# Ten merge gates computed between the mixers and kept in DRAM, with the first block of each layer and the change of layers reordered, in a two-layer hybrid backbone

## The chip, the cores and the metric

The kernel runs on one core of one Trainium2 chip. The metric is the device time of one execution in microseconds (us). A TensorE product of two float32 numbers is made of three products of rounded halves here: each operand is split into a rounded part (H) and the residue (L), and H·H, H·L and L·H are summed in PSUM.

## The reference, cut to what matters

512 latent tokens and 256 context tokens of width 1024 pass two layers. Each layer does the following; the last layer leaves the context alone after the mixers.

```python
shift, scale, gate = _modulation(c, w_ada, b_ada)      # silu(cond) @ w_ada + b_ada
h = _rms_norm(x, norm_g) * (1.0 + scale) + shift       # the same for the context, with c_ctx
(... gla ..., ... hgrn ..., ... attention ..., mg) = _split_in(jnp.matmul(h, w_in))
# three mixers: chunked GLA (4 heads), chunked HGRN (8 heads), windowed attention (8 heads)
y = jnp.stack(ys, axis=2)
proj = jnp.einsum('btnw,nwd->btnd', y, w_branch)       # one projection per branch
gates = jax.nn.sigmoid(mg.reshape(mg.shape[:-1] + (N_BRANCH, D_MODEL)))
merged = jnp.sum(gates * proj, axis=2)
x_new = x + gate * jnp.matmul(merged, w_out)
```

The 24 gates of a layer (3 branches of 8 blocks of 128 channels) depend on h alone. A branch projection depends on all of its mixer's output y.

## The kernel before

The activations lie transposed, channels on the 128 partitions and tokens in the free dimension: 8 blocks of 128 channels by 768 tokens (512 latent, then 256 context). `hH` and `hL` hold the normalized, modulated input of a layer. The weights come as 304 blocks of 128 output channels (512 KB each): `wload` (L704) brings a block into one of three `raw` buffers, `wsplit` (L710) writes its two halves into one of three places of `wring`, and `take` and `ahead` (L762, L772) issue this for up to three blocks ahead of the product. `proj_T` (L782) is one block's projection: 24 products of 512 columns for the latents and, where the context is needed, 24 of 256 columns. `proj_V` (L800) makes token-major values.

**The order of the work** is written out by `make_plan` (L74) as a list of jobs, which the loop at the end of `build` runs one after the other. A job named x is the function `j_x`. In a layer: `start`, the four GLA heads, four pairs of HGRN heads, the attention (values `av`, keys `ak`, then for each of four pairs of heads two queries `aq`, two gate projections `ag` and `arun`), then the merge. The merge goes branch by branch. `mg` (L1643) is a gate: a projection of h and a sigmoid into a buffer. `yload` (L1636) queues the loads of that branch's y, which the mixers have stored in DRAM. `yneed` (L1656) waits until they are loaded and split. `br` (L1663) is a branch projection, multiplied by its gate and added up in `merged`. Branch 0 has its eight gates, then eight branch projections; branches 1 and 2 have four and four, twice. After that come eight `out` jobs (L1710) with the residual sum, which also gather the sum of squares for the next layer.

**Queues.** Every engine works off its instructions in the order in which the program issues them. All loads and stores are issued on SyncE's (SP's) queue, a store (`Emit.store`, L386) as well as a load (`Emit.load`, L376). The mixers' recurrences and attention blocks (`rec_head` L927, `att_block` L1213) are background generators. `pace` (L675) advances them while a projection is issued: it keeps estimated times for each engine (`Emit`, L301) and steps a generator as long as VectorE's or ScalarE's estimate is less than 3 us ahead of TensorE's. A step that needs a buffer when none may be had (`Slots`, L267, 40 buffers of 768 columns, with a reserve for work that has begun) forces other generators on (`on_full`, L682); `need` (L692) does so until one is done. The y loads (`yload_`, L1620) are generators in the same queue, behind the attention blocks.

**Activation tables.** Exp and Ln share one table; Silu and Sigmoid have others. `Emit.act` (L406, instruction at L420) counts a change of table, and loads appear in the trace as ACT_TABLE_LOAD at L402 or L420.

**The beginning** (`j_start` L1329, layer 0). The modulation of block k needs `cond_mm(k)` (L1366, a product of the conditioning with 1 MB of weights), a copy out of PSUM, and `cond_cols(k)` (L1380, a product with two columns, then two small sums on VectorE). Then `make_h` (L906) makes `hH` and `hL` of the block: for the latents and then for the context a scaled product (stt, L447), an activation into `hH` (L420) and another stt into `hL` (L447). The blocks' turns are interleaved so:

```python
for k in range(KT):
    cond_mm(k + 2)
    products(k)          # both weight blocks, latents and context
    cond_cols(k + 2)
    make_h(l, k + 2, xs[k + 2], rs)
```

**The change of layers.** Of the modulation of layer 1, 20 of the 24 blocks are made during the merge of layer 0 on VectorE: a job `adp` puts a weight block of `w_ada` into the stream of weights, and `ada_dots` (L747) forms its dot products with the conditioning (L502). Blocks 16 to 19 are made after the last `out` by four `ads` jobs (L1691): 8 products of two columns each (`ada_mm`, L860), two passes a product. Between them stand the root of the sum of squares (`SumSq.rstd`, L898) and `make_h` of the first five blocks. `j_start` of layer 1 makes the other three, splits the value weights of the first GLA head (`split_v`, L1422) and does the first key and query projections; `j_gvl` (L1466) then uses these value weights.

## Time and profile before

| | us |
|---|---|
| median of 3 runs | 2730.41 |
| lowest, highest | 2730.09, 2734.94 |
| the profiled execution | 2726.76 |
| its span | 2725.0 |
| TensorE busy (PE) | 2634.3, 97% |
| its weight loads (PEld) | 2333.5, 86% |
| VectorE busy (DVE) | 1762.1, 65% |
| ScalarE busy (ACT) | 1104.0, 41% |
| GpSimd busy (POOL) | 169.9, 6% |

The profiled execution is one run, and its span is the part of it between the first and the last instruction. Busy time counts from an instruction's start to its end; matmuls overlap in the pipeline, so their durations are longer than their spacing. A wait in square brackets behind an instruction is the idle time of its engine before it and what ended it. PEclk is the granted clock of TensorE as a share of 2.4 GHz.

### The profile page before, as it was taken

To read this page: it belongs to the slowest core of one execution; us is meant where nothing else is said; L and a number is where in the kernel's file an instruction comes from. 1 tells how busy PE (TensorE), PEld (TensorE's weight loads), DVE (VectorE), ACT (ScalarE), POOL (GpSimd) and SP (SyncE) were. 2 spreads that over 40 slices of the span, in tenths; PEclk is the share of its full clock that TensorE was granted. 3 is DMA by queue.
4 is the path that set the end of the run, shared out by engine and by line. 5 is a ranking of instruction groups with operands and counts; after the bars stand their busy time and mean duration, and the time that the engine had idled before them with its cause. 6 is when DMAs were issued, how large, how long until landed. Compare 5 with 4: busy or idle time off the path is not lost. (4 is left out here: it accounts for less than half of the span.)

```text
span 2725.0 us, 40634 instructions
## 1 busy us (share of the span) xinstructions
PE 2634.3 (97%) x16050; PEld 2333.5 (86%) x16050; DVE 1762.1 (65%) x3562; ACT 1104.0 (41%) x2029; POOL 169.9 (6%) x425
## 2 busy tenths in 40 slices
PE   7999999999999999999999899999999899979998
PEld 5999989988988888888888798888989788868886
DVE  5566657686787766854555456667787887754454
ACT  4444433444334555211211344445565446652122
POOL 0000002001020100000000000001001110000000
PEclk9999999999999999999999899999999999989999
DMA  7111111111111112542423311212121122124333
GB/s 257 48 58 59 59 59 49 57 50 64 59 41 51 45 52 78 173 155 93 139 85 124 124 51 59 74 55 67 59 76 53 45 68 76 63 66 140 102 116 108
DMA packets 87038, 221.91 MB, mean 81 GB/s; under 512 B 9664, under 2 KB 31168, under 8 KB 86848
## 3 DMA queue, kind: packets, MB, share of 16 engines
q1 hardware_dynamic: 86848, 219.32, 24.1%
q8 instruction: 126, 2.06, 0.3%
q14 instruction: 64, 0.52, 0.1%
HBM read 199.36 MB, written 19.92 MB: 80 GB/s over the span
## 5 line engine op out<-in xcount | busy, mean ns | idle before, releaser
L514 PE MATMUL acc<-hH,wring 128*128 128x512 f32 (+1 forms) x5056 | 1398.8, 356 | 8.9 <-ACT hH L420 7.5
L514 PEld LDWEIGHTS acc<-hH,wring 128*128 128x128 f32 x5056 | 897.7, 190 | 137.5 <-ACT hH L420 11.6
L514 PE MATMUL acc<-hL,wring 128*128 128x512 f32 (+1 forms) x2528 | 882.6, 351 | 0.0
L514 PEld LDWEIGHTS acc<-hL,wring 128*128 128x128 f32 x2528 | 478.9, 190 | 57.4 <-DVE hL L447 1.3
L514 PE MATMUL mx<-s,s 128*128 128x256 f32 (+4 forms) x2576 | 397.2, 302 | 26.2 <-ACT s L462 8.7
L514 PEld LDWEIGHTS mx<-s,s 128*128 128x128 f32 (+1 forms) x2576 | 354.1, 195 | 47.8 <-ACT s L462 11.1
L431 DVE TENSOR_TENSOR wring<-raw,wring 128x1024 fp32r<-128x1024 f32 x268 | 329.3, 1234 | 28.6 <-ACT wring L462 19.1
L514 PE MATMUL acc<-s,wring 128*128 128x512 f32 (+1 forms) x1728 | 334.6, 355 | 2.4 <-POOL s L431 1.4
L514 PEld LDWEIGHTS acc<-s,wring 128*128 128x128 f32 x1728 | 286.2, 190 | 49.4 <-POOL s L431 2.6
L420 ACT ACTIVATE s<-s 128x768 f32<-128x768 f32 (+1 forms) x318 | 258.6, 822 | 137.6 <-DVE s L447 88.1
L514 PE MATMUL acc<-wring,hH 128*128 128x256 f32 x1536 | 286.4, 285 | 0.0
L462 ACT CAST wring<-raw 128x1024 fp32r<-128x1024 f32 x167 | 173.3, 1047 | 277.1 <-PE acc L514 237.5
L431 DVE TENSOR_TENSOR s<-s,s 128x768 f32<-128x768 f32 (+4 forms) x278 | 232.0, 851 | 63.8 <-ACT s L420 42.8
L514 PEld LDWEIGHTS acc<-wring,hH 128*128 128x128 f32 x1536 | 242.3, 192 | 0.3
L514 PE MATMUL acc<-wring,hL 128*128 128x256 f32 x768 | 217.2, 283 | 0.0
L420 ACT ACTIVATE s<-acc 128x768 f32<-128x768 f32 (+2 forms) x112 | 76.5, 683 | 275.0 <-PE acc L514 250.3
L431 DVE TENSOR_TENSOR s<-s,fb 128x128 f32<-128x128 f32 (+2 forms) x610 | 183.3, 359 | 0.7
L460 DVE CAST wring<-raw 128x1024 fp32r<-128x1024 f32 x109 | 75.6, 694 | 129.1 <-PE acc L514 127.7
L514 PEld LDWEIGHTS acc<-wring,hL 128*128 128x128 f32 x768 | 147.3, 192 | 0.2
L462 ACT COPY s<-mx 128x256 f32<-128x256 f32 (+2 forms) x191 | 67.5, 378 | 191.2 <-PE mx L514 132.6
L530 PE MATMUL mx<-const,s 128*128 128x128 f32 (+1 forms) x732 | 112.9, 279 | 26.5 <-DVE s L431 16.4
L431 DVE TENSOR_TENSOR s<-s,acc 128x768 f32<-128x768 f32 (+1 forms) x48 | 39.4, 820 | 139.8 <-PE acc L514 139.8
(110 smaller groups left out, 2200.7 us busy)
## 6 DMA issues: line engine op xcount, KB each, us to landing
raw<-in_W SPq DMA_DIRECT2D x304, 512.0 KB, 3.3
y<-s SPq DMA_DIRECT2D x80, 128.0 KB, 1.7
s<-y SPq DMA_DIRECT2D x24, 384.0 KB, 5.9
s<-in_xT SPq DMA_DIRECT2D x16, 384.0 KB, 4.5
s<-in_wada SPq DMA_DIRECT2D x16, 384.0 KB, 7.2
s<-y SPq DMA_DIRECT2D x24, 256.0 KB, 4.6
y<-s SPq DMA_DIRECT2D x80, 64.0 KB, 1.6
s<-in_wvl SPq DMA_DIRECT2D x8, 288.0 KB, 7.1
```

The lines of the kernel that those rows point to most:

```text
L420: self.nc.scalar.activation(out, in_, func, **kw)
L431: (self.nc.vector if e == 'v' else self.nc.gpsimd).tensor_tensor(out, a, b, op=op)
L460: self.nc.vector.tensor_copy(out, in_)
L462: self.nc.scalar.copy(out, in_)
L514: self.nc.tensor.matmul(out, lhsT=lhsT, rhs=rhs, start=start, stop=stop)
L530: self.nc.tensor.transpose(out, in_, ident)
```

## The change

- Gates: a new job `mgx` computes a gate as `mg` does, stores the result in DRAM on SP's queue and frees the buffer. In layer 0, gates 0 and 1 of branch 0 stand between the queries and the gate projections of the third and the fourth pair of attention heads, one each. In layer 1, gates 0 to 3 of branch 0 stand before the attention values, and 4 to 7 two each in the third and fourth pair. `yneed` loads them back.
- Merge: in layer 1 the eight gates of branch 1 now stand before the projections of branch 0, four gates of branch 2 before the eight projections of branch 1, and the first half of branch 2 has no gates before it. In layer 0 the order is as before without the two gates; the y loads of branch 0 come first.
- All 24 modulation blocks of layer 1 are made by dot products in the merge of layer 0; the `ads` jobs, their weights (`wads`) and `ada_mm` go. Two dot blocks stand behind each of the first eight branch projections, one behind each of the others.
- `make_h` is divided into `make_h1` (both scaled products, in place, then both activations) and `make_h2` (both residues), which is issued one block later. In layer 0 a block's products are divided by weight block, with the modulation product of block k+2 between.
- The last `out` of layer 0 makes its latents first, with their sum of squares and root while TensorE makes the context; `start` of layer 1 does all eight blocks of the latents, then of the context. The value weights are loaded and split during the last four `out` jobs.
- Loads at the beginning: a weight block, a modulation block, a weight block, then the rest; the value weights stand ahead of the third weight block. The sum of squares is closed once less.

```diff
+    def mgx(l, nd):
+        job(l, 'mgx', nd, win('mg', 8 * nd[0] + nd[1]))
...
+        early = [(0, d) for d in range(2 if ctx else 8)]
+        spilled = set(early)
+        if not ctx:
+            for _ in range(4):
+                mgx(l, early.pop(0))
...
+            for _ in range(0 if p < 2 else 1 if ctx else 2):
+                mgx(l, early.pop(0))
...
+        cond = [(l, i) for i in range(16, 24)] + [(l + 1, i) for i in range(24)] if ctx else []
+        if ctx:
+            steps = [(0, [(0, d) for d in range(8)], range(8)), (1, [(1, d) for d in range(4)], range(4)),
+                     (1, [(1, d) for d in range(4, 8)], range(4, 8))]
+        else:
+            steps = [(0, [(1, d) for d in range(8)], range(8)), (1, [(2, d) for d in range(4)], range(8))]
+        steps += [(2, [(2, d) for d in range(4)], range(4)), (2, [(2, d) for d in range(4, 8)], range(4, 8))]
+        gated, begun = set(spilled), set()
+        for br, gates, ds in steps:
+            for nd in gates:
+                if nd not in gated:
+                    gated.add(nd)
+                    job(l, 'mg', nd, win('mg', 8 * nd[0] + nd[1]))
+                if br not in begun:
+                    begun.add(br)
+                    job(l, 'yload', br)
+            if br not in begun:
+                begun.add(br)
+                job(l, 'yload', br)
+            job(l, 'yneed', (br, ds))
+            for d in ds:
+                job(l, 'br', (br, d), (f'br{br}', d))
+                for _ in range(2 if len(cond) > 16 else 1):
+                    if cond:
+                        adp(*cond.pop(0))
+            if ds[-1] == 7:
+                job(l, 'yfree', br)
...
+        def part(self, j, q, r):
+            t0, m = self.parts[j]
+            mm(self.ps[j], ones, q[:, t0:t0 + m], start=False, stop=True)
+            if r is not None:
+                self.root(j, r)
+        def root(self, j, r):
+            t0, m = self.parts[j]
+            act(r[:, t0:t0 + m], self.ps[j], AF.Ln, scale=1.0 / D, bias=eps)
+            act(r[:, t0:t0 + m], r[:, t0:t0 + m], AF.Exp, scale=-0.5)
         def rstd(self):
             self.close(True)
-            r = self.acc
-            for ps, (t0, m) in zip(self.ps, self.parts):
-                act(r.ap[:, t0:t0 + m], ps, AF.Ln, scale=1.0 / D, bias=eps)
-            act(r.ap, r.ap, AF.Exp, scale=-0.5)
-            return r
-    def make_h(l, k, x, r):
-        t = arena.alloc(NT)
-        for j, (t0, n) in enumerate(((0, NL), (NL, NC))):
-            sl = slice(t0, t0 + n)
-            shift = ada[l][:, k, j:j + 1]
-            stt(t.ap[:, sl], x.ap[:, sl], amod[l][:, k, j:j + 1], r.ap[:, sl], ALU.mult, ALU.mult)
-            act(hH[k][:, sl], t.ap[:, sl], AF.Identity, bias=shift, scale=1.0)
-            stt(hL[k][:, sl], t.ap[:, sl], shift, hH[k][:, sl].bitcast(F32), ALU.add, ALU.subtract)
-        t.free()
-        x.free()
+            for j in range(len(self.parts)):
+                self.root(j, self.acc.ap)
+            return self.acc
...
+    PARTS = ((0, NL), (NL, NC))
+    def make_h1(l, k, x, r, parts=(0, 1)):
+        for j in parts:
+            sl = slice(PARTS[j][0], sum(PARTS[j]))
+            stt(x.ap[:, sl], x.ap[:, sl], amod[l][:, k, j:j + 1], r.ap[:, sl], ALU.mult, ALU.mult)
+        for j in parts:
+            sl = slice(PARTS[j][0], sum(PARTS[j]))
+            act(hH[k][:, sl], x.ap[:, sl], AF.Identity, bias=ada[l][:, k, j:j + 1], scale=1.0)
+    def make_h2(l, k, x, parts=(0, 1)):
+        for j in parts:
+            sl = slice(PARTS[j][0], sum(PARTS[j]))
+            stt(hL[k][:, sl], x.ap[:, sl], ada[l][:, k, j:j + 1], hH[k][:, sl].bitcast(F32), ALU.add, ALU.subtract)
+        if 1 in parts:
+            x.free()
...
             for k in range(KT):
+                if k < 2:
+                    wload(st['loaded'])
+                    st['loaded'] += 1
                 load(k)
+            load_v(l)
...
+                sq.add(x.ap, k in (1, 3, 5))
...
+        if l == 0:
+            for k in range(KT):
+                make_h2(l, k, xs[k])
+                if k == 1:
                     load_rest()
+                if k == KT - 1:
+                    ahead()
+                products(k, js=(0,))
                 if k + 2 < KT:
                     cond_mm(k + 2)
-            elif k + 5 < KT:
-                make_h(l, k + 5, xs[k + 5], rs)
-            if k == 3:
-                load_v()
-            if k == KT - 1:
-                ahead()
-            if k >= 4:
-                split_v()
-            products(k)
-            if l == 0 and k + 2 < KT:
-                cond_cols(k + 2)
-                make_h(l, k + 2, xs[k + 2], rs)
+                products(k, js=(1,))
+                if k + 2 < KT:
+                    cond_cols(k + 2)
+                    make_h1(l, k + 2, xs[k + 2], rs)
+                if k >= 3 and raw_v:
+                    split_v()
+        else:
+            tail = S0.pop('tail')
+            for part in range(2):
+                make_h1(l, 0, xs[0], rs, (part,))
+                if part == 0:
+                    tail[0]()
+                for k in range(KT):
+                    if k + 1 < KT:
+                        make_h1(l, k + 1, xs[k + 1], rs, (part,))
+                    make_h2(l, k, xs[k], (part,))
+                    if part and k == KT - 1:
+                        ahead()
+                    products(k, (part,))
+                    if part == 0 and k in (0, 2):
+                        tail[1 + k // 2]()
...
+    def j_mgx(l, nd):
+        j_mg(l, nd)
+        s = S_['sig'].pop(nd)
+        S_['spill'][nd] = t = tc.dram_tile([P, S_['nt']], F32, name=f"g{l}_{nd[0]}_{nd[1]}")
+        nc.sync.dma_start(out=t, in_=s.ap)
+        s.free()
...
+    def j_yneed(l, arg):
+        n, ds = arg
+        for d in ds:
+            if (n, d) in S_['spill']:
+                S_['sig'][n, d] = s = arena.alloc(S_['nt'])
+                E.load(s.ap, S_['spill'].pop((n, d)))
...
+        if ctx and d == KT - 1:
+            return last_out(l, d, xr)
+        if ctx and d == 3:
+            load_v(l + 1)
         ps = proj_T(take(), hH, hL, ctx)
+        if ctx and d > 3:
+            split_v()
...
+    def last_out(l, d, xr):
+        sq = S0['sq']
+        i = take()
+        psA, psB = acc()[:, 0:NL], mx()[:, 0:NC]
+        q, r = arena.alloc(NT), arena.alloc(NT)
+        E.t['pe'] = max(E.t['pe'], wready[i])
+        def residual(j, ps):
+            t0, m = PARTS[j]
+            x = xr.ap[:, t0:t0 + m]
+            stt(x, ps, ada[l][:, 16 + d, j:j + 1], x, ALU.mult, ALU.add)
+            act(q.ap[:, t0:t0 + m], x, AF.Square)
+        for j, ps in enumerate((psA, psB)):
+            t0, m = PARTS[j]
+            k = 0
+            for kt in range(KT):
+                for w, x in ((WH(i), hH), (WH(i), hL), (WL(i), hH)):
+                    mm(ps, w[:, kt], x[kt][:, t0:t0 + m], start=(k == 0), stop=(k == 3 * KT - 1))
+                    k += 1
+                if j == 0 and kt == 1:
+                    ahead()
+                if j == 1 and kt == 4:
+                    sq.part(0, q.ap, r.ap)
+            if j == 0:
+                E.table(COMBINED)
+                residual(0, psA)
+                split_v()
+                sq.close()
+        def square():
+            residual(1, psB)
+        def total():
+            sq.part(1, q.ap, None)
+            q.free()
+        def norm():
+            sq.root(1, r.ap)
+        S0['tail'] = square, total, norm
+        S0['rs'] = r
+        x_in[l + 1].append(xr)
```

## Rows read from the trace of the kernel before

**Rows 1.** Busy time in stretches: stretch, length, busy per engine (instructions), clock, DMA, GB/s
```profile
0.00:61.26 61.26, 47.26 (x283) 28.95 (x283) 35.12 (x76) 28.89 (x50) 0.20 (x4) 0.97 0.76 277
...
870.00:1100.00 230.00, 221.21 (x1457) 198.51 (x1456) 157.91 (x363) 124.44 (x295) 14.35 (x6) 0.99 0.19 61
1100.00:1518.90 418.90, 418.90 (x2411) 370.67 (x2409) 238.78 (x448) 69.97 (x78) 0.00 (x0) 1.00 0.39 133
1518.90:1564.14 45.24, 36.26 (x170) 28.18 (x168) 24.30 (x43) 17.71 (x29) 0.00 (x0) 0.85 0.22 75
...
2148.00:2165.80 17.80, 10.44 (x71) 9.53 (x70) 15.33 (x43) 6.54 (x21) 3.67 (x14) 0.81 0.00 1
2165.80:2416.70 250.90, 245.39 (x1484) 214.30 (x1483) 187.88 (x425) 142.38 (x315) 13.09 (x20) 0.99 0.21 68
2416.70:2455.10 38.40, 23.83 (x106) 18.33 (x106) 16.45 (x42) 16.58 (x39) 3.75 (x3) 0.73 0.25 80
2455.10:2713.70 258.60, 257.95 (x1136) 212.93 (x1136) 122.32 (x148) 58.55 (x73) 0.00 (x0) 1.00 0.33 112
```
**Rows 2.** Timeline of PE, beginning: start, duration, instruction, idle before it
```profile
38.23 0.61 PE L514 MATMUL mx<-const,s 128*128 128x2 f32 x4 [0.66 <-ACT s L462]
...
42.81 0.61 PE L514 MATMUL mx<-const,s 128*128 128x2 f32 x4 [0.66 <-ACT s L462]
43.34 1.07 PE L526 MATMUL mx<-s,cs 128*32 128x256 f32 x16
```
**Rows 3.** Timeline of DVE, the same turn of the beginning
```profile
43.84 0.75 DVE L447 SCALAR_TENSOR_TENSOR s<-s,amod,s 128x512 f32<-128x512 f32 x1
45.39 0.75 DVE L447 SCALAR_TENSOR_TENSOR hL<-s,ada,hH 128x512 fp32r<-128x512 f32 x1 [0.79 <-ACT hH L420]
46.06 0.48 DVE L447 SCALAR_TENSOR_TENSOR s<-s,amod,s 128x256 f32<-128x256 f32 x1
```
**Rows 4.** Timeline of DVE, change of layers: two sums back to back
```profile
1533.46 0.48 DVE L447 SCALAR_TENSOR_TENSOR hL<-s,ada,hH 128x256 fp32r<-128x256 f32 x1 [0.57 <-ACT hH L420]
1533.86 0.74 DVE L447 SCALAR_TENSOR_TENSOR s<-s,amod,s 128x512 f32<-128x512 f32 x1
```
**Rows 5.** Timeline of PE, change of layers
```profile
1521.66 1.45 PE L514 MATMUL mx<-s,const 128*128 128x512 f32 x4
...
1528.58 6.82 PE L514 MATMUL mx<-cs,s 128*128 128x2 f32 x32
...
1564.14 0.40 PE L514 MATMUL acc<-s,hH 128*128 128x288 f32 x1 [3.01 <-ACT s L462]
```
**Rows 6.** Timeline of ACT, change of layers: root of the latents' sum
```profile
1527.97 0.69 ACT L420 ACTIVATE s<-mx,eps 128x512 f32<-128x512 f32 x1 [4.09 <-PE mx L514]
```
**Rows 7.** Timeline of DVE, merge of layer 0: same dot product, one turn apart
```profile
1130.75 0.95 DVE L502 CUSTOM_DVE_ANT_0 s<-raw,s 128x768 f32<-128x768 f32 x1
...
1139.16 0.95 DVE L502 CUSTOM_DVE_ANT_0 s<-raw,s 128x768 f32<-128x768 f32 x1
```
**Rows 8.** Timeline of PE, end of the HGRN heads of layer 1
```profile
2158.54 4.51 PE L514 MATMUL mx<-s,s 128*128 128x128 f32 x24 [6.28 <-DVE s L494]
```
**Rows 9.** Timeline of PE, after the last gate product of layer 1
```profile
2419.94 0.66 PE L530 MATMUL mx<-const,s 128*128 128x128 f32 x4 [2.23 <-ACT s L420]
...
2434.88 2.42 PE L530 MATMUL mx<-const,s 128*128 128x128 f32 x10 [3.05 <-DVE s L443]
2442.28 0.58 PE L514 MATMUL mx<-s,s 128*128 128x256 f32 x1 [4.98 <-ACT s L462]
```
**Rows 10.** Chain that ended last, before the first branch products of layer 1
```profile
2436.80 3.68 DMA s<-y
```
**Rows 11.** Page, DMA issues: count, KB each, median us from issue to landing
```profile
s<-y SPq DMA_DIRECT2D x24, 256.0 KB, 4.6
```
**Rows 12.** Timeline of ACT, attention of layer 1
```profile
2399.74 1.28 ACT L420 ACT_TABLE_LOAD   x1
2401.03 0.60 ACT L420 ACTIVATE s<-acc 128x512 f32<-128x512 f32 x1
```

More of the change, by code (lines that the diff above doesn't have):

```diff
@@ L156, in make_plan @@
         assert not cond
-        if ctx:
-            for i in range(16, 20):
-                job(l + 1, 'ads', i)
         job(l, 'end')
@@ L858, in build @@
     lcd = e0
-    def ada_mm(ps, w):
-        for kt in range(KT):
-            mm(ps, w(kt), cs[:, 2 * kt:2 * kt + 2], start=(kt == 0), stop=(kt == KT - 1))
     def ada_mod(l, k, n=1):
@@ L1324, in begin_layer, with load_v, split_v @@
         S_.update(l=l, ctx=ctx, nt=NT if ctx else NL, z={}, q={}, k={}, v={}, f={}, g={}, sig={}, merged={},
-                  kHL={}, qHL={}, y={}, last=[],
+                  kHL={}, qHL={}, y={}, last=[], spill={},
                   yd=[[tc.dram_tile([P, NT], F32, name=f"y{l}_{n}_{k}") for k in range(KT)] for n in range(3)])
         S_['blocks'] = [(b, True) for b in range(4)] + ([(4, False), (5, False)] if ctx else [])
+    raw_v = []
+    def load_v(l):
+        for j in range(0, KT, 2):
+            raw_v.append(arena.alloc(576))
+            E.load(raw_v[-1].ap.rearrange("p (a b) -> p a b", b=288), A['wvl'][l][:, j:j + 2])
+    def split_v():
+        raw = raw_v.pop(0)
+        hl = [arena.alloc(576, True) for _ in range(2)]
+        E.split(hl[0].r, hl[1].r, raw.ap)
+        raw.free()
+        S0.setdefault('wvl', []).append([b.r.rearrange("p (a b) -> p a b", b=288) for b in hl] + hl)
     def j_start(l, arg):
@@ L1392, in j_start @@
         if l == 0:
-            for _ in range(2):
-                wload(st['loaded'])
-                st['loaded'] += 1
             for k in range(KT):
+                if k < 2:
+                    wload(st['loaded'])
+                    st['loaded'] += 1
                 load(k)
+            load_v(l)
             loads()
@@ L1406, in j_start @@
                 cond_cols(k)
-                make_h(l, k, xs[k], rs)
+                make_h1(l, k, xs[k], rs)
         else:
@@ L1413, in j_start, with products @@
         parts = [((0, NL), (NL, NC)), ((0, NL), (NL, NC))[:2 if S_['ctx'] else 1]]
-        raw_v = []
-        S_['wvl'] = []
-        def load_v():
-            for j in range(0, KT, 2):
-                raw_v.append(arena.alloc(576))
-                E.load(raw_v[-1].ap.rearrange("p (a b) -> p a b", b=288), A['wvl'][l][:, j:j + 2])
-        def split_v():
-            raw = raw_v.pop(0)
-            hl = [arena.alloc(576, True) for _ in range(2)]
-            E.split(hl[0].r, hl[1].r, raw.ap)
-            raw.free()
-            S_['wvl'].append([b.r.rearrange("p (a b) -> p a b", b=288) for b in hl] + hl)
-        def products(kt):
+        def products(kt, of=(0, 1), js=(0, 1)):
             E.t['pe'] = max(E.t['pe'], wready[i + 1])
-            for j in range(2):
+            for j in js:
                 for w, x in ((WH(i + j), hH), (WH(i + j), hL), (WL(i + j), hH)):
                     for t0, n in parts[j]:
+                        if (t0 > 0) not in of:
+                            continue
                         c = count[j][t0 > 0]
@@ L1729, in j_out @@
         S0['sq'].add(xr.ap)
-        if ctx and d > 4:
-            ads_load(11 + d)
         x_in[l + 1].append(xr)
@@ L1734, in j_out @@
             nc.sync.dma_start(out=x_dram[l + 1][d], in_=xr.ap[:, 0:NL])
+    def last_out(l, d, xr):
[35 more added lines that the diff above has]
+        x_in[l + 1].append(xr)
+        nc.sync.dma_start(out=x_dram[l + 1][d], in_=xr.ap[:, 0:NL])
     def j_end(l, arg):
@@ L1744, in build @@
     jobs = dict(start=j_start, gvl=j_gvl, gk=j_gk, gz=j_gz, gv=j_v, gq=j_gq, gg=j_g, grun=j_grun, hv=j_v, hf=j_hf, hq=j_hq,
-                hg=j_g, hrun=j_hrun, av=j_av, ak=j_ak, aq=j_aq, ag=j_g, arun=j_arun, yload=j_yload, mg=j_mg,
-                yneed=j_yneed, br=j_br, yfree=j_yfree, adp=j_adp, ads=j_ads, out=j_out, end=j_end)
+                hg=j_g, hrun=j_hrun, av=j_av, ak=j_ak, aq=j_aq, ag=j_g, arun=j_arun, yload=j_yload, mg=j_mg, mgx=j_mgx,
+                yneed=j_yneed, br=j_br, yfree=j_yfree, adp=j_adp, out=j_out, end=j_end)
     for l, name, arg, blocks in plan:
```

55 lines of the change are left out of this document (6 added, 49 removed).

## The prediction

> **What bounds the kernel now.** I read three views in this order. First, busy time in consecutive stretches [rows 1]: where does TensorE (PE), which works nearly all the time, stand still or run on the lower clock? Only there can a change win. It idles 14.0 us of the first 61.26, 8.8 in attention of layer 0 (870 to 1100), 9.0 of 45.24 where the layers change, 7.4 of 17.8 where the HGRN heads of layer 1 end, 5.5 in its attention, and 14.6 of 38.4 between its last gate product and its first full branch product. Both merges (1100 to 1519, 2455 to 2714) have PE full at granted clock 1.00: 418.90 us for 2411 products are 8.34 for a block of 48 in layer 0, and 258.60 for 1136 are 5.46 for a block of 24 in layer 1, so a product of 512 columns takes 0.228 and one of 256 columns 0.120. Where PE idles the clock falls as well: 0.85, 0.81 and 0.73 mean that part of the stretch ran at 1.2 instead of 2.4 GHz. Second, the timeline of each such stretch, engine by engine, for what is waited for; last, single instructions, for prices.
>
> **The beginning.** Per block k of the normalized input, PE does a modulation product (about 1.0 us), a two-column product that finishes the modulation (0.53 from start to start) and six pairs of projection products (0.35 a pair). One turn takes 4.58 us, from 42.81 back to 38.23 [rows 2]. Its chain: the two-column product, then on VectorE (DVE) and ScalarE (ACT) the four scaled sums of make_h with two activations between them, alternating, then the ACT copy for the next two-column product. The change takes the residue hL out of this chain but puts it elsewhere: make_h2(k) is issued after make_h1(k+1), and make_h1(k+1) waits for the two-column product of k+1, which PE does just before the projection of k. So PE must wait for an hL that cannot begin until then. Counted from the start of the two-column product [rows 2 to 4]: 1.03 us to the first sum (42.81 to 43.84), 0.67 and 0.40 for the two sums (start to start), 0.75 for hL of the latents and 0.04 for the signal make 2.89. hL of the context follows 0.40 later and its product is done at 3.41; the last pair of this half (0.35), the modulation product (1.0) and the other half (three pairs, 1.05) give 5.81 until the next two-column product. That is 1.23 longer than now. Five turns lie between the two-column products of k=2 and k=7: +6.2. Two of them also get a split of the value weights on DVE in front of hL (about 1.1 each): +2.2. The swap of weight and modulation loads and one closing of the sum of squares less move the first turn by under 1 us either way; I take 0. So the change **lengthens the beginning by 8 us**. Bounds: +3, if the turns overlap more than this order suggests; +12, if a stretch of lower clock falls in (3 us of PE work per turn would double).
>
> **The change of layers.** Now 45.24 us pass from the end of the latent half of the last output block (1518.90) to the first value product (1564.14) [rows 1]. In them lie the 64 two-column products of the modulation blocks 16 to 19, half of them at the lower clock and 6.82 us long, and the wait of 3.01 for the copy out of PSUM behind weight splits [rows 5]. All that goes: those blocks become dot products in the merge, and the value weights are split during the output blocks. What remains, laid on the engines: PE closes the sum of squares (1.45) and does 15 context products (1.8) and the ones product of the latents (two thirds of 1.45), 4.2; two activations of 0.69 [rows 6] bring the latents' norm to 5.6; first sum, activation and hL to 7.9. After that each k costs DVE two latent sums, 1.34, and PE six products, 1.37, so eight take 10.9, and the norm product of the context adds 0.4: 19.2. The context half is DVE's, 16 sums at 0.40 [rows 4], 6.4 us, of which some overlap: 24. The copy out of PSUM makes it 25. **Saved: 20 us.** Bounds: 22 if nothing waits; 10 if the whole latent half falls to the lower clock, as the products there do now in part.
>
> **The four dot blocks.** A branch block of layer 0 takes PE 8.34 us; with two dot blocks DVE's turn is 8.41 [rows 7]. Four such turns stand in branch 0 now, eight afterwards. DVE falls behind 0.07 per turn, half a microsecond in all, and PE has a spare PSUM buffer: 0, at most +3 if the weight casts go to DVE too.
>
> **The ten gates.** Their products are only moved: eight of layer 1 and two of layer 0, 60 us in all, leave merges where PE is full and enter mixers where it is not. The gain is the idle time and the low-clock time that they fill, no more. Each also carries its weight split, its sigmoid with up to two table loads, a store on SP's queue and later a load. SP waits there for the sigmoid, and the weight loads and y stores issued after it queue behind; weights are loaded at least three blocks ahead, 16 us against at most one gate, so 0, with +2 as the other end.
> - Four gates stand before the attention values of layer 1. There PE waits 6.28 us in one piece for a predicated copy [rows 8], because the new buffers force the recurrences to go on first. DVE is the busy engine in that stretch (15.3 of 17.8), so I take 6 of 7.4 idle plus about 2 of low clock: **-6**, bounds 0 and -9.
> - Four gates between query and gate products of the third and fourth pairs of heads, 21.8 us of PE work. They let the attention blocks run ahead, so that less is left when the last eight gates are done. Now the rest of it leaves PE waiting 2.23, 3.05, 4.98 us and more [rows 9], and the first y tiles, loaded only then, put 3.68 of transfer on the chain of waits [rows 10]. 14.6 idle, some 7 of low clock and 5 at a similar stall earlier are there; the table loads, the attention blocks' own latency and eight gate tiles that are reloaded ahead of y eat part: **-15**, bounds -4 and -23.
> - Two gates in layer 0: of 8.8 idle I take a third, **-3**, bounds 0 and -7.
>
> **The last branch of layer 1** loses its cover. Its y tiles are loaded behind four gate products now; afterwards the first branch product stands right behind the loads. A 256 KB load lands after 4.6 us [rows 11]. If the loads pass the queue early, only the splits show (+2); if they wait for the buffers of the branch before, 4.6 of transfer, cast and difference of the first tile and the lower clock after the pause come to +10. I take **+4**, near the lower end: of 40 buffers 8 hold sums, 4 gates and 16 y tiles, so twelve are free by then.
>
> **Sum.** 8 - 20 - 6 - 15 - 3 + 4 = -32. The profiled execution took 2726.76 us (span 2725.0 and 1.76 around it), so 2694.8 by its own measure; it lies 3.65 below the median of the three runs shown, 2730.41, and I state medians: **2698**. A measurement of this kernel can tell about 0.2%, 5.5 us, from no change.
>
> **Rivals.** (1) The gates fill nothing: the planner advances the background only by its own clock, and a gate's buffer forces the same recurrence steps as the attention values do now, so the stalls just move, and the change does not do there what it says. For it: 5.5 us of idle in layer 1's attention lie between products that should cover them. Against it: the stalls before branch 0 stand where no product is left to issue. 8 - 20 + 4 = -8: 2722.
> (2) Everything fills and the beginning hardly grows: 4 - 21 - 9 - 22 - 6 + 2 = -52: 2678. Against it is the order of hL above.
> (3) Slower: the moved sigmoids put ACT on the chain. Place: the mixers of layer 1 and the end of layer 0's, where the attention blocks use exponentials. Price: a load of 1.28, a sigmoid of 0.60 and a load back [rows 12], 3.2 us per gate, 32 for ten; with no idle filled 8 - 20 + 4 + 32 = +24: 2754. It decides against the change once more than 8 of those 32 stand on the chain while nothing else is gained. Against it: ACT is busy 142 of 251 us there [rows 1], and a sigmoid may wait. The rows show the sigmoid starting 0.01 us behind the load's end.
> The Trainium skill (ScalarE: Activation LUTs, What ACT_TABLE_LOAD costs) states about 1380 ns of drain beside the 1283 of the load for every switch; twenty switches would be some 53 us and this rival would give about 2782, an estimate from that page. The trace does not agree with that drain: none shows.
>
> **Chances.** Forecast 0.66, its own range 2686 to 2712; rival 1 0.17, 2 0.12, 3 0.05. The range 2680 to 2722 leaves out rival 3, half of 1 and half of 2, 0.195. Faster by over 0.2% are the forecast, rival 2 and two thirds of 1: 0.90; the rest of rival 1 is 0.05, rival 3 0.05.
>
> **What would show it.** Right: two-column products 5.8 us apart in the beginning with PE waiting for hL; the first value product of layer 1 about 25 us after the latent half of the last output block; no wait above 3 us before the attention values and before branch 0 of layer 1; a new wait of some 4 us at the last branch. Wrong: a beginning of 61 us, a low clock through the change of layers, or the same idle sums in the mixers with the gates moved.

## The result, and the profile after

| | before | after |
|---|---|---|
| median (us) | 2730.32 (4 runs) | 2700.89 (4 runs, 2699.6 to 2705.36) |
| ratio | 1 | 0.9889, 95% interval 0.9877 to 0.9901 |
| span of the profiled execution | 2725.0 | 2697.8 |
| PE busy | 2634.3 | 2617.0 |

The change gains 29.4 us; 2698 was forecast. The same view as [rows 1], with its stretches moved to where the same work now lies (columns as there):

```profile
0.00:76.70 76.70, 53.43 (x279) 30.99 (x280) 38.16 (x86) 26.75 (x46) 0.20 (x4) 0.87 0.62 227
885.00:1115.00 230.00, 225.83 (x1502) 204.06 (x1501) 155.34 (x360) 125.12 (x300) 9.56 (x4) 0.99 0.21 66
...
1531.04:1556.96 25.92, 21.84 (x106) 17.52 (x104) 21.55 (x40) 15.41 (x27) 0.00 (x0) 0.93 0.13 46
2126.00:2166.50 40.50, 36.99 (x204) 31.27 (x203) 27.65 (x70) 18.83 (x40) 5.44 (x17) 0.96 0.21 66
2166.50:2427.00 260.50, 250.04 (x1524) 218.67 (x1523) 193.75 (x431) 140.67 (x323) 15.02 (x22) 0.99 0.22 72
2427.00:2466.40 39.40, 38.25 (x203) 31.82 (x202) 23.91 (x46) 19.12 (x37) 2.60 (x2) 1.00 0.37 122
```

The first value product stands at 76.65 instead of 61.26, and the clock of the beginning is 0.87 instead of 0.97. The change of layers takes 25.92 instead of 45.24. In front of branch 0 of layer 1 PE idles 1.15 of 39.40 us at full clock, where it idled 14.6 of 38.4 at 0.73. But the attention of layer 1 now has 10.5 us of idle in 260.50, where it had 5.5 in 250.90: some of the waiting only moved.

One turn of the beginning, timeline of all engines (compare [rows 2, 3]):

```profile
29.35 0.50 PE L533 MATMUL mx<-const,s 128*128 128x2 f32 x4
...
29.89 0.16 DVE L450 TENSOR_TENSOR ada<-mx,cols 128x4 f32<-128x4 f32 x1 [4.80 <-PE mx L533]
...
30.28 1.15 DVE L466 SCALAR_TENSOR_TENSOR s<-s,amod,s 128x512 f32<-128x512 f32 x2
...
31.07 1.12 ACT L439 ACTIVATE hH<-s,ada 128x512 fp32r<-128x512 f32 x2 [2.37 <-DVE s L466]
31.35 1.14 DVE L466 SCALAR_TENSOR_TENSOR hL<-s,ada,hH 128x512 fp32r<-128x512 f32 x2
...
32.15 0.78 PE L533 MATMUL acc<-hL,wring 128*128 128x512 f32 x2 [1.84 <-DVE hL L466]
...
35.38 0.50 PE L533 MATMUL mx<-const,s 128*128 128x2 f32 x4
```

The chain is the forecast one. DVE stands still 4.80 us until PE has done the two-column product of the next block; then come its two sums, only then hL of the present block, and PE waits 1.84 for that. The turn is 6.03 us (5.81 was forecast, 4.58 before). What was not in the sum is the clock, here PE alone in 25 us each (busy, clock, DMA, GB/s):

```profile
25.00:50.00 25.00, 19.28 (x128) 0.87 0.91 329
50.00:75.00 25.00, 16.19 (x79) 0.75 0.00 1
```

Change of layers, timeline of PE (compare [rows 5]): the two-column products of blocks 16 to 19 are gone, and three short waits are left.

```profile
1538.13 0.49 PE L533 MATMUL acc<-hH,wring 128*128 128x512 f32 x1 [1.92 <-ACT hH L439]
1539.09 0.50 PE L533 MATMUL acc<-hL,wring 128*128 128x512 f32 x1 [0.47 <-DVE hL L466]
...
1556.96 0.40 PE L533 MATMUL acc<-s,hH 128*128 128x288 f32 x1 [1.65 <-ACT s L481]
```

To compare kernels I cut every profiled execution at the same PE instructions. The times in the table are differences of their starts, in us. **B**: from 0 to the first value product. **M0**: from the end of the layer's value products to the first branch product of layer 0, which always holds eight gate products. **C**: from there to the first value product of layer 1. **M1**: from the first 256-column value product of layer 1 to the end of its branch 0; where eight gate products stand in it instead of sixteen, I added 8 x 5.46 = 43.7, eight blocks at the price worked out from [rows 1], and marked it with a +.

| kernel | median | B | M0 | C | M1 |
|---|---|---|---|---|---|
| before | 2730.3 | 61.3 | 1040.6 | 442.8 | 940.8+ |
| after | 2700.9 | 76.7 | 1037.6 | 423.4 | 919.8 |
| residual first | 2679.7 | 54.7 | 1036.6 | 423.4 | 923.3 |
| old beginning | 2685.1 | 63.7 | 1036.2 | 423.4 | 920.2 |
| old order of loads | 2702.8 | 79.7 | 1039.6 | 423.4 | 923.3 |
| filled | 2695.9 | 72.7 | 1034.7 | 423.7 | 924.4 |
| none before the values | 2699.6 | 79.7 | 1036.5 | 423.4 | 918.9 |
| none in the pairs | 2705.9 | 79.9 | 1036.2 | 423.4 | 924.6 |
| none in layer 0 | 2707.8 | 78.0 | 1044.8 | 423.4 | 922.1 |
| change of layers alone | 2712.9 | 62.4 | 1043.8 | 423.8 | 943.9+ |
| all in the merge | 2686.1 | 54.8 | 1034.5 | 423.5 | 928.4 |
| old merge order | 2701.0 | 53.4 | 1036.0 | 423.4 | 946.1+ |
| third gate, first residual | 2670.2 | 51.9 | 1026.6 | 429.6 | 920.1 |

Columns that an edit leaves alone still scatter: B by 3 us among kernels with the beginning of after, M0 by 5, M1 by some 5; in the beginning the stretches at the lower clock fall differently from one execution to the next. A single profile decides nothing below that.

### The profile page after: what moved, and what is told of

Read it like the earlier page. It is cut to its first block, busy times and chain, and to the rows that moved or that the text cites. A ratio compares the mean times of both kernels' runs of the same rounds, so it can differ in the third digit from the quotient of the medians.

```text
span 2697.8 us, 40579 instructions
## 1 busy us (share of the span) xinstructions
PE 2617.0 (97%) x15982; PEld 2318.4 (86%) x15982; DVE 1767.1 (66%) x3592; ACT 1105.6 (41%) x2037; POOL 168.9 (6%) x426
## 5 line engine op out<-in xcount | busy, mean ns | idle before, releaser
L533 PE MATMUL mx<-s,s 128*128 128x256 f32 (+4 forms) x2576 | 389.5, 299 | 12.9 <-DVE s L513 4.4
L533 PEld LDWEIGHTS mx<-s,s 128*128 128x128 f32 (+1 forms) x2576 | 348.4, 192 | 32.8 <-issue 7.1
L481 ACT CAST wring<-raw 128x1024 fp32r<-128x1024 f32 x173 | 179.7, 1048 | 276.9 <-PE acc L533 182.9
L450 DVE TENSOR_TENSOR s<-s,s 128x768 f32<-128x768 f32 (+5 forms) x279 | 234.0, 855 | 67.0 <-ACT s L439 45.9
L481 ACT COPY s<-acc 128x768 f32<-128x768 f32 (+2 forms) x129 | 87.8, 681 | 101.0 <-PE acc L533 98.9
L549 PE MATMUL mx<-const,s 128*128 128x128 f32 (+1 forms) x732 | 109.1, 275 | 15.7 <-DVE s L450 14.6
```

What stands on the lines that cost most here:

```text
L450: (self.nc.vector if e == 'v' else self.nc.gpsimd).tensor_tensor(out, a, b, op=op)
L481: self.nc.scalar.copy(out, in_)
L533: self.nc.tensor.matmul(out, lhsT=lhsT, rhs=rhs, start=start, stop=stop)
L549: self.nc.tensor.transpose(out, in_, ident)
```

## The experiments

**The beginning.** First, hL taken out of the chain: `e1a_residual_first` issues it ahead of the next block's sums.

```diff
+            make_h2(l, 0, xs[0])
             for k in range(KT):
-                make_h2(l, k, xs[k])
...
                 products(k, js=(1,))
+                if k + 1 < KT:
+                    make_h2(l, k + 1, xs[k + 1])
                 if k + 2 < KT:
                     cond_cols(k + 2)
                     make_h1(l, k + 2, xs[k + 2], rs)
```

> Only the beginning of layer 0 is edited: the residual of block k+1 (make_h2) is issued before cond_cols(k+2) and make_h1(k+2) and no longer behind them; load order, halves and gates stay. Theory (the order puts hL into the chain of one turn, and the low clock is a consequence): the waits of 1.84 to 3.00 us for hL go, the clock holds, the first value product falls from 76.7 to 58..63 us and the whole time by 14 to 18 us, to about 2685. Rival A (the interleaved loads of weights and modulation blocks cost it): no change, within 3 us of 2701. Rival B (DVE simply has too much to do in the beginning, whatever the order): 2696 to 2701, with the wait for hL turned into a wait for the copy of the modulation product.

2679.68 us, ratio to before 0.9808 (0.9792 to 0.9824): 21.2 below the changed kernel and B at 54.7, both beyond the stated ranges. The timeline of the same turn:

```profile
33.57 0.50 PE L533 MATMUL mx<-const,s 128*128 128x2 f32 x4
...
34.50 1.15 DVE L466 SCALAR_TENSOR_TENSOR s<-s,amod,s 128x512 f32<-128x512 f32 x2
...
35.28 1.12 ACT L439 ACTIVATE hH<-s,ada 128x512 fp32r<-128x512 f32 x2 [2.64 <-DVE s L466]
...
36.48 0.31 PEld L533 LDWEIGHTS acc<-hL,wring 128*128 128x128 f32 x2
36.60 0.53 PE L533 MATMUL acc<-hL,wring 128*128 128x512 f32 x2
36.62 0.74 DVE L466 SCALAR_TENSOR_TENSOR hL<-s,ada,hH 128x512 fp32r<-128x512 f32 x1
```

The hL products at 36.60 have no bracket behind them: their hL has been there since the turn before, and the one that DVE begins at 36.62 is the next. Five turns in a row take 3.74 to 3.77 us, less than the 4.58 of before. Most of the difference is the wait of 0.66 for the copy in [rows 2], which is gone: the new order of the products puts work of PE between the modulation product and the two-column product. With the residual first the new loop is 5.4 us faster than the old one (2685.07, next). So it was the place of make_h2 that cost time, not the rest of the loop.

Second, the old loop with all else as after (`e1b_old_beginning`):

```diff
             for k in range(KT):
-                make_h2(l, k, xs[k])
                 if k == 1:
                     load_rest()
+                if k + 2 < KT:
+                    cond_mm(k + 2)
                 if k == KT - 1:
                     ahead()
+                if k >= 4:
+                    split_v()
-                products(k, js=(0,))
-                if k + 2 < KT:
-                    cond_mm(k + 2)
-                products(k, js=(1,))
+                products(k)
                 if k + 2 < KT:
                     cond_cols(k + 2)
-                    make_h1(l, k + 2, xs[k + 2], rs)
+                    make_h(l, k + 2, xs[k + 2], rs)
-                if k >= 3 and raw_v:
-                    split_v()
```

> The loop of the beginning is put back: sums, activation and residual of a block in one piece, products of both weights whole behind the modulation product, splits ahead of the products from k = 4. The new order of loads, the change of layers and the gates stay. Theory: the first value product is back at 60 to 63 us, the whole time 13 to 17 us lower, about 2686. Rival A (loads): 2698 to 2704. If this comes out lower than the residual-first kernel, the split of the products in halves costs something too.

2685.07 (2684.34 to 2686.13), so the new loop, as the change has it, costs 15.8 us; B is 63.7, just above the range. Third, the loads (`e1c_old_loads`):

```diff
+            for _ in range(2):
+                wload(st['loaded'])
+                st['loaded'] += 1
             for k in range(KT):
-                if k < 2:
-                    wload(st['loaded'])
-                    st['loaded'] += 1
                 load(k)
```

> Only the order of the loads is put back (both weight blocks before the first modulation block). Theory: the first value product stays at 75.5 to 78 us and the time within 3 us of the changed kernel's. Rival A (the loads cost the 15 us): first value product at about 62 us, time near 2686.

2702.75 (2698.04 to 2708.16), within 3 us of the changed kernel; B at 79.7 is above the stated 78, but within its scatter. The order of the loads is not the cause. Fourth, what the clock alone costs (`e2_filled`):

```diff
+            FILL = (0, 5, 5, 5, 5, 9, 9, 9)
             for k in range(KT):
                 make_h2(l, k, xs[k])
...
+                if 0 < k < KT:
+                    fill = mx()
+                    for _ in range(FILL[k]):
+                        mm(fill[:, 0:NL], WH(i)[:, k], hH[k][:, 0:NL])
                 products(k, js=(0,))
```

> In each turn of the beginning from k = 1 on, 5 products of 128x512 (9 from k = 5 on; 47 in all, 10.8 us at full clock) that nobody reads are put in front of the projection products, where PE waits for hL; it tells what the lower clock costs by itself. Theory (order about 8, clock about 7): with the clock held the two-column products stand 6.0 us apart (7.1 with a split), the first value product comes at 69 to 72 us, the time falls by 4 to 8 us. Rival C (the lower clock costs nothing, since PE only waits longer for the same hL): first value product at 76 to 80 us, time 0 to 4 us higher. Rival D (the clock is the whole of it): first value product near 62 us, time near 2686.

2695.89 (2694.36 to 2696.95): 5.0 us faster with 47 more products. Timeline of PE, one turn with a split:

```profile
48.18 0.50 PE L533 MATMUL mx<-const,s 128*128 128x2 f32 x4
48.54 1.40 PE L533 MATMUL mx<-hH,wring 128*128 128x512 f32 x5
49.78 0.50 PE L533 MATMUL acc<-hH,wring 128*128 128x512 f32 x2
52.15 0.78 PE L533 MATMUL acc<-hL,wring 128*128 128x512 f32 x2 [1.87 <-DVE hL L466]
...
55.38 0.50 PE L533 MATMUL mx<-const,s 128*128 128x2 f32 x4
```

and the same 25 us for PE alone (busy, clock, DMA, GB/s):

```profile
50.00:75.00 25.00, 21.20 (x132) 1.00 0.08 23
```

At full clock a turn takes 6.02 or 6.03, and 7.2 with a split in front of hL (48.18 to 55.38). The five turns between the two-column products of k=2 and k=7 take 33.3 us (29.29 to 62.57), against 37.7 in after (29.35 to 67.03) and 23.4 before (29.17 to 52.54). But the first of the five, 6.84 us (29.29 to 36.13), still ran partly on the lower clock, here PE from 30 to 35:

```profile
30.00:35.00 5.00, 5.00 (x29) 0.65 1.03 396
```

Three turns of 6.03 and two of 7.2 make 32.5 us, an estimate of the five at full clock. So the order costs 9.1 and the lower clock 5.2 on top; 1.0 of B's 15.4 lies behind the last of them. The clock was a consequence of the waits, and it had a price of its own: with the residual first, where the waits are gone, it is 1.00 from 30 us on.

**The gates of layer 1.** Each set of four by itself, made in the merge instead (`e3a_none_before_values`, then `e3b_none_in_pairs`):

```diff
         if not ctx:
-            for _ in range(4):
-                mgx(l, early.pop(0))
+            early, spilled = early[4:], set(early[4:])
...
-            steps = [(0, [(1, d) for d in range(8)], range(8)), ...
+            steps = [(0, [(0, d) for d in range(4)] + [(1, d) for d in range(8)], range(8)), ...
```

> The four gates in front of the attention values of layer 1 are not made early: gates (0,0) to (0,3) are made in the merge, ahead of the gates of branch 1, and stay on chip; all else stays (four gates in the third and fourth pair). Theory (gates gain what PE idles at their place, independently of each other): 5 us slower (3 to 8), and the wait for the predicated copy of 6 us stands in front of the attention values again. Rival (their gain is only that the recurrences get on earlier and the later gates would get it anyway): within 2 us of the changed kernel.

2699.62 (2697.92 to 2701.36): no loss, as the rival had it. The wait for the predicated copy is back in front of the values, as in [rows 8], yet M1 is 918.9. Timeline of PE:

```profile
2151.18 4.40 PE L532 MATMUL mx<-s,s 128*128 128x128 f32 x24 [6.29 <-DVE s L512]
```

```diff
-        early = [(0, d) for d in range(2 if ctx else 8)]
+        early = [(0, d) for d in range(2 if ctx else 4)]
...
-            for _ in range(0 if p < 2 else 1 if ctx else 2):
+            for _ in range(0 if p < 2 else 1 if ctx else 0):
```

(with gates (0,4) to (0,7) put into the merge's first step as above)

> The four gates between query and gate products of the third and fourth pair of layer 1 are not made early: gates (0,4) to (0,7) are made in the merge, ahead of the gates of branch 1; the four before the attention values stay. Theory: PE again has too little left when the last attention block ends; 15 us slower (10 to 18). Rival (the twelve gate products ahead of branch 0 now cover the attention blocks as the moved ones do): within 4 us.

2705.87 (2701.57 to 2707.18): 5.0 slower, not 15, just past the rival's 4, and its runs overlap with those of the changed kernel (2699.6 to 2705.36). The terms don't add. In both kernels, sixteen gate products still stood ahead of branch 0, since the merge's new order puts the eight of branch 1 there. The next two kernels take the two things apart, on the residual-first kernel: no early gate but all sixteen ahead (`e5_all_in_merge`), and early gates but none of branch 1 ahead (`e6_old_merge_order`).

```diff
-        early = [(0, d) for d in range(2 if ctx else 8)]
+        early = [(0, d) for d in range(2 if ctx else 0)]
...
-        if not ctx:
-            for _ in range(4):
-                mgx(l, early.pop(0))
...
-            for _ in range(0 if p < 2 else 1 if ctx else 2):
+            for _ in range(1 if ctx and p > 1 else 0):
...
-            steps = [(0, [(1, d) for d in range(8)], range(8)), ...
+            steps = [(0, [(0, d) for d in range(8)] + [(1, d) for d in range(8)], range(8)), ...
```

> On the residual-first kernel (2679.7 us): no gate of layer 1 is made early or kept in DRAM; all sixteen gates of branches 0 and 1 are made in the merge ahead of branch 0. Either set of four taken out by itself had cost 0 and 5 us only. First theory (the gates gain by filling PE's idle time in the mixers, so all eight out lose all of it): 16 to 21 us slower, about 2698. New theory (what counts is how many products are left to do while the last attention blocks end and the first y tiles land; the eight gates of branch 1 that the new order of the merge puts ahead of branch 0 give most of it, wherever the others stand): within 6 us, 2678 to 2686.

2686.06 (2681.93 to 2687.62): 6.4 slower, just outside the 6 of the new theory and far from the first. Timeline of PE, the two long waits:

```profile
2124.66 0.55 PE L530 MATMUL mx<-s,s 128*128 128x128 f32 x1 [6.28 <-DVE s L510]
...
2424.65 0.79 PE L530 MATMUL acc<-hH,wring 128*128 128x512 f32 x1 [7.62 <-ACT s L436]
```

and of ACT, in front of the second:

```profile
2419.95 1.24 ACT L478 CAST s<-s 128x512 fp32r<-128x512 f32 x2 [4.65 <-DMA s<-y]
2422.82 1.28 ACT L478 CAST s<-s 128x512 fp32r<-128x512 f32 x2 [1.63 <-DMA s<-y]
2424.00 0.59 ACT L436 ACTIVATE s<-acc 128x512 f32<-128x512 f32 x1
```

PE waits for a sigmoid to empty the PSUM buffer, and the sigmoid is queued on ACT behind casts of y tiles that have not landed. The profile names ACT; the cause is the transfer behind it.

```diff
-        if ctx:
+        if True:
             steps = [(0, [(0, d) for d in range(8)], range(8)), ...
```

> On the residual-first kernel (2679.7 us): the eight early gates of layer 1 stay where the change put them, but the merge of layer 1 goes in the old order: no gate of branch 1 stands ahead of branch 0, which so begins right behind the attention. First theory (the gain lies in the mixers): the attention blocks are done early, and only the first y tiles show, 3 to 7 us slower. New theory (the cover ahead of branch 0 counts): 15 to 25 us slower, with waits of 10 us and more in front of the first product of branch 0.

2701.01 (2700.23 to 2704.05): 21.3 slower. Timeline of PE:

```profile
2383.82 0.97 PE L549 MATMUL mx<-const,s 128*128 128x128 f32 x6 [2.72 <-DVE s L462]
2387.07 0.69 PE L549 MATMUL mx<-const,s 128*128 128x128 f32 x2 [2.28 <-ACT s L439]
...
2403.43 1.75 PE L549 MATMUL mx<-const,s 128*128 128x128 f32 x6 [2.41 <-ACT s L439]
...
2415.74 0.50 PE L533 MATMUL acc<-s,wring 128*128 128x512 f32 x1 [2.84 <-ACT s L481]
...
2423.78 3.65 PE L533 MATMUL acc<-s,wring 128*128 128x512 f32 x7 [2.59 <-ACT s L481]
```

With nothing else to issue, PE steps through the last attention blocks at their pace and then waits for y tiles. No single wait is the 10 us that I had written; the loss is many of 2 to 3, and from 2340 to 2427 PE is busy 68.47 of 87.00 us at clock 0.88. By M1: eight gates ahead of branch 0 in all 940.8 and 943.9, or 946.1 where they were made early; sixteen, all late, 928.4; sixteen, eight of them early, about 922. These are single profiles, but the runs agree: 21.3 us without the eight of branch 1 ahead, 6.4 with all sixteen late. **The number of products ahead of branch 0 is worth 14 of the 20 us, their place in the mixers 6, and early gates without the new order of the merge nothing.**

**Layer 0, and the terms together.** The two gates of layer 0 (`e3c_none_layer0`):

```diff
-        early = [(0, d) for d in range(2 if ctx else 8)]
+        early = [(0, d) for d in range(0 if ctx else 8)]
...
-            for _ in range(0 if p < 2 else 1 if ctx else 2):
+            for _ in range(0 if p < 2 or ctx else 2):
```

> The two early gates of layer 0 are made in the merge again; all else stays. Theory: 3 us slower (0 to 5), the start of branch 0 of layer 0 later by this. Rival (nothing is filled there): within 1 us by the profile.

2707.76 (2706.85 to 2710.0), 6.9 slower, above the stated 5. Timeline of PE; in after these waits are absent from the fourth pair, where a gate stands:

```profile
1019.88 0.44 PE L549 MATMUL mx<-const,s 128*128 128x128 f32 x2 [0.49 <-ACT s L439]
1023.48 0.63 PE L549 MATMUL mx<-const,s 128*128 128x128 f32 x4 [1.42 <-DVE s L450]
...
1026.71 2.93 PE L533 MATMUL mx<-s,s 128*128 128x256 f32 x12 [1.55 <-ACT s L439]
```

The same waits one pair earlier are still there in after, inside the product of the third pair's early gate (944.5 to 966.4):

```profile
960.44 0.63 PE L549 MATMUL mx<-const,s 128*128 128x128 f32 x4 [1.43 <-DVE s L450]
...
963.68 2.93 PE L533 MATMUL mx<-s,s 128*128 128x256 f32 x12 [1.55 <-ACT s L439]
```

So a gate doesn't fill the waits at its own place.

The change of layers alone (`e4_change_alone`: the old loop of the beginning as above, `early = []`, the old order of the merge in layer 1):

```diff
-        early = [(0, d) for d in range(2 if ctx else 8)]
+        early = []
...
-        if ctx:
+        if True:
             steps = [(0, [(0, d) for d in range(8)], range(8)), ...
```

> The loop of the beginning is put back and no gate is made early, with the merge of layer 1 in the old order; what is left of the change is the change of layers, the modulation products of blocks 16 to 19 as dot products, and the order of loads. Theory (terms add): 2730 - 20 = 2710, 2707 to 2713; from the end of the latent half of the last output block to the first value product of layer 1 about 26 us. Rival (part of the 20 is given back where the merge of layer 0 is left with more dot products and the gates' idle hid it): 2716 or more.

2712.91 (2712.12 to 2713.86), 19.4 below its runs of before (2732.26). So the parts, by runs: change of layers -19.4; gates and merge order -27.8 (2712.9 to 2685.1); beginning +15.8. They sum to -31.4, against -29.4 measured. This is no test of whether the terms add: the parts are steps of one chain of kernels, and the difference of 2 us is that between two medians of before (2732.26 and 2730.32).

**Beyond both kernels.** The merge of layer 0 in the order of layer 1 (`e7_layer0_as_layer1`):

```diff
-        if ctx:
+        if False:
             steps = [(0, [(0, d) for d in range(8)], range(8)), ...
...
-            steps = [(0, [(1, d) for d in range(8)], range(8)), ...
+            steps = [(0, [(0, d) for d in range(8)] + [(1, d) for d in range(8)], range(8)), ...
```

> On the residual-first kernel (2679.7 us): the merge of layer 0 goes in the order that layer 1 has after the change, all gates of branches 0 and 1 ahead of branch 0 (the two early ones stay early). Theory: in layer 0 PE waits only 2.4 us once in front of branch 0, so there is little left to cover: 0 to 4 us faster. Rival (the y tiles of branch 1 lose their cover, or sixteen gate tiles of 768 columns take the buffers from the attention blocks): 3 us or more slower, with a new wait inside the merge of layer 0.

2681.19 (2677.31 to 2683.94), no difference from 2679.68 that can be told: layer 0 has little in front of branch 0 to cover. Last, a third early gate in layer 0 and the first residual issued sooner (`e8_best`):

```diff
-        early = [(0, d) for d in range(2 if ctx else 8)]
+        early = [(0, d) for d in range(3 if ctx else 8)]
...
-            for _ in range(0 if p < 2 else 1 if ctx else 2):
+            for _ in range(min(p, 1) if ctx else 0 if p < 2 else 2):
...
                 cond_mm(k)
+                if k == 1:
+                    make_h2(l, 0, xs[0])
                 cond_cols(k)
```

> On the residual-first kernel (2679.7 us): a third early gate in layer 0, in the second pair of heads, where its trace shows waits of 0.53, 1.43 and 1.55 us and the lower clock behind them; and the residual of block 0 is issued ahead of the sums of block 1, which takes away the wait of 1.84 us at 25.05. Theory (a gate in layer 0 gains what PE idles at its place; the residual first helps the first turn as it did the others): 2 to 4 us in the pairs and 1 to 3 us in the beginning, 2672 to 2677. Rival (the count of gates ahead of branch 0 decides in layer 0 as in layer 1, and is the same here): the stretch from the first value products to branch 0 within 1 us, time 2677 to 2680.

2670.17 (2667.61 to 2670.42), ratio to before 0.9775 (0.9762 to 0.9789), the fastest kernel of the study and below the stated 2672 to 2677. B falls by 2.8. M0 falls by 10: the gate stands in the second pair, and the waits of the third pair are gone. (The expectation has them in the second pair; in the residual-first kernel they lie inside the product of the third pair's early gate.) But C gives 6.2 back. Branch 0 now begins at 1098.01, before its last y tile has landed (1098.88), and PE waits inside it. Timeline of PE, then of DVE:

```profile
1106.74 3.57 PE L533 MATMUL acc<-s,wring 128*128 128x512 f32 x13 [3.45 <-DVE s L450]
```

```profile
1098.16 0.95 DVE L521 CUSTOM_DVE_ANT_0 s<-raw,s 128x768 f32<-128x768 f32 x1
...
1104.60 1.23 DVE L450 TENSOR_TENSOR wring<-raw,wring 128x1024 fp32r<-128x1024 f32 x1
1105.74 0.95 DVE L450 TENSOR_TENSOR s<-s,s 128x768 fp32r<-128x768 f32 x1
```

The last line is that tile's split. On ACT its cast stood behind the cast of a weight block that waited 2.25 us for its load; on DVE its split stood behind the dot products of two modulation blocks and a weight split. So 3.8 of the gate's gain is left; the rest of the 9.5 us is M1, which this edit does not touch and which lies within its scatter.

## Why the prediction was right, and where it was not

The total was right, 2700.9 for 2698, but partly by luck: the beginning cost 7.8 us more than forecast, the gates and the merge order gained 7.8 more (27.8 for the 20 of their four terms).

- **Beginning, +8: failed in size.** It cost 15.8. The mechanism was the forecast one. At full clock the turn is 6.03 for 5.81, a split adds 1.17 for 1.1, and the five turns cost 9.1 for 8.4; the two-column product of k=2 comes at 29.35 for 29.17, so the first turn was rightly left out. The step that failed is the clock: the term held none, and its upper bound of +12 only one stretch, where it came back turn after turn (5.2 us in three of the five turns).
- **Change of layers, -20: right**, -19.4; 25.9 us from the end of the latent half to the first value product, for 25.
- **Dot blocks, 0: right.** C falls by 19.4, all of it the change of layers.
- **Gates of layer 1, -6 and -15: the sum was right, the cause wrong.** M1 falls by 21.0 in after, but four gates taken back cost 0 and at most 5.0. I had priced each place by the idle time that lay there. What that time needed was work ahead of branch 0, and the eight gates of branch 1 that the merge's new order puts there give 14 of 20. I had read this edit only as the loss of the last branch's cover. The waits that I said would go also partly moved, as rival 1 had it: 2.32 in front of the values and 3.95 in the pairs, both for an activation that empties a PSUM buffer. Timeline of PE, after:

```profile
2157.61 0.50 PE L533 MATMUL acc<-hH,wring 128*128 128x512 f32 x1 [2.32 <-ACT s L439]
...
2284.40 0.79 PE L533 MATMUL acc<-hH,wring 128*128 128x512 f32 x1 [3.95 <-ACT s L439]
```

- **Gates of layer 0, -3: too small.** 6.9 by runs, at the bound of -7, though a single pair of profiles gave 3.0. Of the idle and the lower clock behind it I had taken only a third.
- **Last branch, +4: wrong.** The loads of y passed SP's queue at 2567.49, eight us before they were wanted, and PE waits 0.52. From the end of branch 0 to the end there are 1.0 us more, eight gates counted as above. The lower bound of +2 was still too high.
- **SP's queue, 0: nothing seen against it on PE.** SP did stand 54.2 us in front of seven of the ten stores until their gate was ready, the longest 17.27, where the forecast set "at most one gate" against 16 us of cover. But no wait of PE above 0.15 us there ends with a weight block. Doubling the stores was not tried.
- **Rival 3** did not come as a whole, but one of its loads stands on a chain. The 2.32 in front of the values ends with a table load of 1.28 and the sigmoids of two moved gates, behind an activation that had waited for GpSimd. The two activations in front of the 3.95 belong to the attention's own gate projections: no merge gate is stored between 2169.66 and 2328.47. Timeline of ACT, after:

```profile
2155.27 0.37 ACT L439 ACTIVATE fb<-fb 128x204 f32<-128x204 f32 x1 [4.31 <-POOL fb L483]
2155.66 1.28 ACT L439 ACT_TABLE_LOAD   x1
2156.96 1.09 ACT L439 ACTIVATE s<-acc 128x512 f32<-128x512 f32 x2
...
2281.62 0.83 ACT L439 ACTIVATE s<-s,sm 128x640 f32<-128x640 f32 x1 [0.49 <-DVE sm L528]
2282.46 1.28 ACT L439 ACT_TABLE_LOAD   x1
2283.75 1.09 ACT L439 ACTIVATE s<-acc 128x512 f32<-128x512 f32 x2
```

  In the Trainium skill (ScalarE: Activation LUTs, What ACT_TABLE_LOAD costs) a drain of about 1380 ns goes with each switch. The trace doesn't agree: both loads take 1.28 us, begin 0.02 and 0.01 us behind the activation before them and are followed by the next within 0.02 us.

What stays open: whether the early gates need to be kept in DRAM at all (a kernel that holds them on chip was not run); how much of M1's remaining idle, 24 us, is the attention blocks' own latency; and whether the sixteen products help by covering the attention blocks or the loads of y, which no run separates.

## What to carry to other kernels

When a chain is cut in two, look at what each half is queued behind in its engine's order: hL left the chain of its own block and joined the next block's, and one moved line was worth 21 us. Before crediting a gain to the place where work was put, count how much independent work stands ahead of the wait in all; sets that can replace each other show little when taken out one at a time. Where PE waits for an eviction, read what that engine had been waiting for before.

## What was not expected of the hardware

- Short waits, one per turn, went with a clock that fell to 1.2 GHz again and again. From 30 to 46 us of after the only waits of PE above 0.1 us are three of 1.84; the granted clock is 1.00 from 30 to 35, then 0.84 and 0.82 in the next two stretches of 5 us. From 50 to 75, with three waits of 3.00, it is 0.75. Before, with waits of 0.65 to 1.23, holds 1.00 from 30 to 60.
- 47 products that nobody reads, put into those waits, held the clock at 1.00 from 35 us on and made the program 5.0 us faster.
- Identical beginnings gave B of 76.7 to 79.9 us in four profiled executions (after, and the three kernels that each take back some gates), the lower clock falling in other places each time.
